# Branch A's product with w_branch_a moved out of the final stage, block by block, and half of w_out kept where h was

## The chip, the cores and the metric

The kernel runs on one core of one Trainium2 chip. The metric is device time in microseconds, the median of several executions. The core's engines are named as the profile names them: PE (TensorE, matrix products; PEld is its loading of weights), DVE (VectorE), ACT (ScalarE), POOL (GpSimd) and SP (SyncE, which here issues all the DMAs). SBUF is the on-chip memory, PSUM the memory that matrix products are written to.

## The reference

One layer of a hybrid encoder runs over a prompt of 2048 rows and a sample of 32 rows, with D_MODEL = 1024. Rows are normalised to h, and one projection of h gives everything else:

```python
qa, ka, va, za, qkv_b, zb, a_b, b_b, gate_a, gate_b = split_projection(x @ w_in)
oa = chunk_band_attention(qa, ka, va, rel_bias)             # branch A, 8 heads of 64
ya = (oa * silu(za)) @ w_branch_a                           # 512 -> 1024
ob, s_new = gated_delta_rule(qb, kb, vb, g, beta, s_prev)   # branch B, 8 heads of 64
yb = (ob * silu(zb)) @ w_branch_b                           # 512 -> 1024
mix = sigmoid(gate_a) * ya + sigmoid(gate_b) * yb
y = layer_norm(ALPHA * x + mix @ w_out, ln_g, ln_b)         # w_out is 1024 x 1024
```

The new keys, values, convolution rows and states are returned as well.

## The kernel before, in words

**Precision.** Products with w_in are made of fp16 pairs (a high and a low part of each operand, three products). Products with w_branch_a, w_branch_b and w_out are made of fp32r pairs in the same way: `hi*hi`, `hi*lo` and `lo*hi`.

**Order of the work.** The rows are done in two halves of 1024. For each half a list of jobs runs on PE (`all_jobs`, line 2051); a job is one 128-column piece of w_in against the half's rows. The jobs feed branch B (`phase_b`, 832), then attention (`phase_a`, 1501), and the last jobs of the second half are the gates of branch A. Each gate's tanh is stored in DRAM (`job_gate`, 813; `sig_dram`), and so are the two branches' gated outputs before their products (`g_dram`). The weights of a job come through two places (`raw_gate`, line 615) filled by `fetch` (618) and split into fp16 pairs by `divide` (662).

**A planner writes the program.** Each step is a Python generator. A small model (`Flow`, 157) gives every operation a cost and every engine a time when it is next free, and always continues the stream whose clock is lowest. Gates, marks and queues (84 to 155) order the streams. What comes out is one fixed list of instructions for each engine, and each engine works its list off in order, so a wait on one instruction holds up all behind it. Since `Engine.__getattr__` issues everything, every compute instruction has line 267 in the profile, and every DMA line 290; they are told apart by the tiles' names.

**The early products.** When the second half's branch B is done, w_branch_b is loaded (`load_w`, 640, called from `fetch`) and `early` (2222) makes branch B's products while attention of the second half runs. The rows are cut into eight blocks of 256 (the last has the 32 sample rows too). One *unit* is one block, one branch and one of eight 128-column pieces f: 12 matmuls (`branch`, 2264). `early` does two blocks at once in one PSUM bank `b`, multiplies by the gate on DVE and stores the result over the gate in `sig_dram`. It takes PE only when the planner sees it idle (line 2240), and it has three gate tiles (`SGB`).

**The final stage.** After the last jobs `fetch` loads w_branch_a to where h was (`hpool`), and `merge` (2278) goes over the blocks. For each f, `unit` makes branch A's product in bank `a` and multiplies by the gate; `fold` adds branch B's stored product and splits the sum into `mh` and `ml`; then four PSUM banks (two row tiles by two column halves, `pj` and `b`) collect 8 x 12 matmuls of 512 columns with w_out (`step`, `low`). A block's w_out products are interleaved with the next block's units (`LAG`). `finish` (2450) takes the banks on DVE, adds the normalised x rows and makes the second LayerNorm. The x rows come through three tiles `xt`: `x_load` (2431) normalises them on DVE and scales and shifts them on POOL, in 16 pieces of 256 columns a pair of tiles and factor.

w_out is split into fp32r pairs by `last_weights` (2099) once attention's memory is free (`fp_open`); it uses the x tiles and the four row vectors' tiles as staging. `q_sg` and `sg_ahead` (2403) load the gates and products through the three `sg` tiles.

**K rows in attention.** `job_k` (1652) writes the last 512 K rows out through one tile `kr`, guarded by `vs_slot`; other intermediates use four places `parts`.

Of the kernel before, what the change touches and what calls it, by code (L numbers as in the profile page):

```python
# [11 lines left out]
F32 = mybir.dt.float32  # L12
# [263 lines left out]
def trunk(ctx: ExitStack, tc: tile.TileContext, x_p, x_s, cache_k, cache_v, st_conv, st_gdn,  # L276
# [338 lines left out]
    raw_gate, w_gate, sig_slots = gate(NRAW), gate(2), gate(2)  # L615
    q_raw, q_w = Queue(flow), Queue(flow)

    def fetch(jobs):

        for job in jobs:  # L620
            if job.half == 1 and job.key == EARLY:
                yield from load_w(1, w_b)
            yield raw_gate
            raw = wpool.tile([P, KD, P], F32, tag="wraw", bufs=NRAW, name="wraw")
# [6 lines left out]
            q_raw.put((job, raw, t))  # L631
            yield

        jobs_near.done()
        yield from load_w(0, w_a)
        for _ in range(NRAW):
            yield raw_gate
        front_w.done()

    def load_w(br, w):  # L640
        yield from claim_w(br)
        for k in range(NP):
            yield raw_gate
            wr = wpool.tile([P, KD, P], F32, tag="wraw", bufs=NRAW, name="wr")
            wr = wr[:].rearrange("p k n -> p (k n)")
            t = dma(wr, w[k * P:(k + 1) * P, :])
            both = [None, raw_gate.give]
            for c in range(2):
                flow.start(split_w(br, k, c, wr[:, c * 512:(c + 1) * 512], t, both[c]))
            yield  # L650
# [11 lines left out]
    def divide():  # L662

        while True:
            job, raw, t = yield from q_raw.get()
# [17 lines left out]
            for i in range(2):  # L683
# [8 lines left out]
                if i:  # L692
                    raw_gate.give()
# [65 lines left out]
    wres, claimed = [None, None], [mark(), mark()]  # L759
# [12 lines left out]
    def split_w(br, k, c, wr, t, give=None):  # L772
        yield claimed[br]
        hi, lo = wres[br]
        yield from split(hi[c][:, k], lo[c][:, k], wr, give, V if k % 2 else G, t, w_ready[br, k, c])

    def claim_w(br):
        if br == 0:
            for g in h_free:
                yield g  # L780
        else:
            yield wr_open
        pool = wr_pool[0] if br else hpool
        names = [f"{x}{c}" for c in range(2) for x in ("hi", "lo")]
        ts = [pool.tile([P, NP, 512], F32R, tag=n, bufs=1, name=f"w{n}{br}") for n in names]
        wres[br] = [ts[0::2], ts[1::2]]
        claimed[br].done()
# [713 lines left out]
    def phase_a(half):  # L1501
# [8 lines left out]
        bias_slots, vs_slot, sample_slot = [gate(2), gate(1)], gate(1), gate(1)  # L1510
        last_block = len(BLOCKS[half]) - 1
        NPART = 4
# [139 lines left out]
        def job_k(k):  # L1652
# [10 lines left out]
            def evac(bi, c0, n, gcol, ps):  # L1663
# [4 lines left out]
                kr = None  # L1668

                def leave():  # L1670
                    nonlocal kr
# [23 lines left out]
                if kr is not None:  # L1695
                    yield from rows_out(kr, kr[:, 0:m], m, nk_p[c0 - (HALF - BAND):c0 - (HALF - BAND) + m], p,
                                        (k.k_s[:], nk_s) if m < n else None)
                    vs_slot.give()
# [227 lines left out]
        def leave_pair(k, t, gt, place):  # L1926
# [16 lines left out]
            at = dma(g_dram[0][k.p][:, cs], ga[:].rearrange("p i n -> p (i n)"))  # L1943
            if t == 6:
# [8 lines left out]
        def sample(k):  # L1953
# [78 lines left out]
            yield dma(g_dram[0][p][:, SEQ:T], ga[:])  # L2032
# [66 lines left out]
    def last_weights():  # L2099

        x_t = []
        for _ in range(3):
            yield x_slots
            x_t.append(fp.tile([P, D], F32, tag="xt", bufs=3, name="wr")[:])
        r_t = [rowv[name][:] for name in ("l0g", "l0b", "lng", "lnb")]

# [6 lines left out]
        def row(name, src):  # L2113
            for c in range(2):
                yield w_ready["o", 3 + list(rowv).index(name), c]
# [11 lines left out]
        stage = x_t + r_t  # L2127
        for i in range(2 * KD):
            if i >= 14:
                yield w_ready["o", 2, i % 2]  # L2130
            yield from load(i // 2, i % 2, stage[i // 2 if i < 14 else 2][:, i % 2 * 512:(i % 2 + 1) * 512])
# [3 lines left out]
        for k in (0, 1, KD - 1):  # L2135
# [11 lines left out]
    g_slot, g_early, x_slots = gate(1), gate(1), gate(3)  # L2147
    q_eg, q_eb, q_es = Queue(flow), Queue(flow), Queue(flow)
    q_eg.low = gate(0)
    early_done, claimed_b = [mark() for _ in range(NB)], {}  # L2150
    SGB = 3
# [5 lines left out]
    q_g, q_x, q_sg = Queue(flow), [Queue(flow), Queue(flow)], Queue(flow)  # L2157
# [21 lines left out]
    def load_g():  # L2179
        yield jobs_near  # L2180
        for b in range(NB):
            yield g_slot
            gs = [get_g(0, b, 0)]
            if not claim_block(b):
                yield g_early
                gs.append(get_g(1, b, 1))
            q_g.put(gs)
            yield

    def claim_block(b):  # L2190

        if b not in claimed_b:
            claimed_b[b] = "merge"
        return claimed_b[b] == "early"

    def early_g():
        yield wr_open
        for some in [[b, b + 1] for b in range(0, NB - 2, 2)] + [[NB - 2], [NB - 1]]:
            if some[0] in claimed_b or fp_open.at is not None:
                break  # L2200
            gs = []
            for i, b in enumerate(some):
                claimed_b[b] = "early"
                place = 1 - (b if len(some) == 1 else i)
                yield (g_slot, g_early)[place % 2]
                gs.append((b, get_g(1, b, place % 2), place % 2))
            q_eg.put(gs)
# [3 lines left out]
    def early_sg():  # L2211
        while True:
            c0, n = yield from q_eb.get()
            for f in range(KD):
                if c0 == SEQ // 2:
                    yield gate_done[1, 1, f]
                yield sg_slots
                sg = sg_tile()
                q_es.put((sg, dma(sg[:, 0:n], sig_dram[1][f][:, c0:c0 + n])))
# [359 lines left out]
```

## Time and profile before

| | |
|---|---|
| median of 3 executions | 2007.88 us (2007.57 to 2008.67) |
| the profiled execution | 2002.91 us, of which 2001.1 us span from first to last instruction |
| PE busy | 1903.8 us (95%) |
| DVE busy | 1410.8 us (70%) |
| ACT busy | 993.7 us (50%) |
| POOL busy | 807.2 us (40%) |
| mean granted TensorE clock | 0.978 |
| DMA | 257.57 MB, mean 129 GB/s |

A row of a group reads: line, engine, operation, tile written <- tiles read, shape, count | busy us, mean ns of one | idle time of the engine just before, and what ended most of it. A busy PE is not PE at its peak: matmuls overlap, so the time of one is read from the distance of their starts. A row of a stage reads: from:to, length, then busy us (and count) of PE, PEld, DVE, ACT and POOL, the granted clock, the busy share of the DMA engines and GB/s.

### The profile page before, as it was taken

The page shows a single profiled execution, that of the slowest core. Times are in us where ns is not written, and L with a number is a line of the kernel's source. Part 1 is how long each engine was busy: PE and PEld are TensorE (multiplying, and loading weights), DVE is VectorE, ACT ScalarE, POOL GpSimd, SP SyncE. Part 2 cuts the span into 40 slices and gives each one's busy share as a digit, 9 for nine tenths or more (in the row PEclk, how much of TensorE's full clock was granted, in tenths as well). Part 3 has the DMA queues.
Part 4 walks back from the last instruction along what each step waited for, and adds up shares of the span by engine and source line. Part 5 has one row for each costly group of instructions (what it writes and reads, how often), then busy time and mean ns, then how long its engine had stood idle before and what let it go on. Part 6 is the DMA issues. An engine that isn't in the chain of part 4 may idle for free.

```text
span 2001.1 us, 40919 instructions
## 1 busy us (share of the span) xinstructions
PE 1903.8 (95%) x14513; PEld 1347.3 (67%) x14513; DVE 1410.8 (70%) x4482; ACT 993.7 (50%) x2022; POOL 807.2 (40%) x1139
## 2 busy tenths in 40 slices
PE   8999999999999999999999999899999897799997
PEld 5455676676454557666676778588877566688885
DVE  7789989873378768589889985455366655676766
ACT  6665545444577777655445444444365764211110
POOL 7344434423344445343334432322132323456664
PEclk8999999999999999999999999999999998899998
DMA  3224232333478885222232342678688867544432
GB/s 132 67 88 128 63 105 67 90 94 97 122 158 197 185 185 141 76 77 80 60 109 65 89 109 75 172 190 207 204 176 201 160 152 189 203 145 136 149 128 78
DMA packets 371861, 257.57 MB, mean 129 GB/s; under 512 B 247106, under 2 KB 314030, under 8 KB 371656
## 3 DMA queue, kind: packets, MB, share of 16 engines
q1 hardware_dynamic: 371656, 254.96, 47.9%
q8 instruction: 114, 1.87, 0.4%
q14 instruction: 91, 0.75, 0.1%
HBM read 148.63 MB, written 63.24 MB: 106 GB/s over the span
## 4 chain that ended last, share of the span: by engine, by line
PE 66%; DVE 19%; ACT 5%; issue 4%; POOL 2%; DMA 2%; SPq 1%; POOLq 0%; DVEq 0%; ACTq 0%
PE pj L267 38%; PE b L267 14%; PE a L267 7%; PE x L267 3%; DVE acc L267 2%; PE c L267 2%; DVE sys_t L267 2%; DVE sys_u L267 2%; PE o L267 2%; DVE kd_bd L267 1%; POOL wlo L267 1%; DVE q_bd L267 1%; ACT whi L267 1%; POOL xt L267 1%; DVE v_t L267 1%
## 5 line engine op out<-in xcount | busy, mean ns | idle before, releaser
L267 PE MATMUL pj<-hi,whi 128*128 128x512 f16 (+2 forms) x1992 | 644.3, 339 | 18.8 <-ACT kr L267 8.9
L267 PE MATMUL pj<-hi,wlo 128*128 128x512 f16 (+2 forms) x1952 | 636.3, 339 | 0.6 <-POOL wlo L267 0.5
L267 PEld LDWEIGHTS <-whi 128*128 128x128 f16 x3984 | 410.0, 105 | 229.7 <-issue 12.3
L267 PE MATMUL pj<-lo,whi 128*128 128x512 f16 (+2 forms) x1992 | 457.0, 340 | 0.0
L267 POOL TENSOR_TENSOR wlo<-wraw,whi 128x256 f16<-128x256 f32 x384 | 268.8, 723 | 445.5 <-ACT whi L267 335.9
L267 PEld LDWEIGHTS <-wlo 128*128 128x128 f16 x1952 | 205.1, 105 | 120.7 <-issue 12.8
L267 ACT ACTIVATE wraw<-wraw,w_scale 128x1024 f32<-128x1024 f32 (+1 forms) x98 | 111.4, 1137 | 81.5 <-DVE w_scale L267 79.9
L267 POOL TENSOR_TENSOR pu<-sb,pu 128x640 f16<-128x640 f32 (+2 forms) x64 | 82.6, 1292 | 168.1 <-ACT pu L267 127.1
L267 ACT ACTIVATE sb<-sb,mx,unit 128x640 f32<-128x640 f32 (+4 forms) x128 | 108.7, 849 | 70.5 <-DVE mx L267 63.6
L267 ACT CAST whi<-wraw 128x512 f16<-128x512 f32 (+1 forms) x196 | 119.2, 610 | 35.2 <-PE pj L267 32.4
L267 DVE TENSOR_TENSOR sys_u<-sys_u,sys_t 128x60 f32<-128x60 f32 (+24 forms) x527 | 124.5, 242 | 5.7
L267 ACT CAST mh<-sg 128x256 fp32r<-128x256 f32 x64 | 25.7, 407 | 206.4 <-DVE sg L267 183.0
L267 DVE SCALAR_TENSOR_TENSOR acc<-raw,cwT,acc 128x512 f32<-128x512 f32 x144 | 112.8, 784 | 8.4 <-ACT acc L267 7.0
L267 DVE TENSOR_TENSOR sys_t<-sys_u,sys_p 128x60 f32<-128x60 f32 (+21 forms) x459 | 110.2, 243 | 5.5
L267 DVE CUSTOM_DVE_ANT_0 sb<-a,bias 128x320 f32<-128x320 f32 (+5 forms) x136 | 66.3, 498 | 50.3 <-PE a L267 48.9
L267 ACT COPY v_t<-o 128x64 f32<-128x64 f32 x132 | 27.8, 210 | 143.5 <-PE o L267 107.0
L267 POOL TENSOR_TENSOR w_scale<-w_scale,mhalf 128x1 f32<-128x1 f32 x49 | 32.1, 655 | 159.1 <-DVE w_scale L267 119.9
L267 PEld LDWEIGHTS <-pt 128*128 128x128 f16 x1680 | 67.3, 99 | 29.7 <-DMA pt<-pu 7.2
L267 ACT CAST pu<-sb 128x640 f16<-128x640 f32 (+4 forms) x128 | 82.0, 649 | 0.5
L267 ACT ACTIVATE sig<-pj,w_half 128x512 f32<-128x512 f32 (+2 forms) x84 | 49.3, 587 | 65.5 <-PE pj L267 60.0
L267 PE MATMUL c<-vt,pt 128*128 128x64 f16 x1680 | 70.9, 194 | 10.7 <-DVE ob L267 5.8
L267 PE MATMUL a<-ghi,whi 128*128 128x256 f32 (+1 forms) x256 | 68.3, 296 | 12.8 <-ACT ghi L267 7.6
(353 smaller groups left out, 4305.3 us busy)
## 6 DMA issues: line engine op xcount, KB each, us to landing
wraw<-in_w_in SPq DMA_DIRECT2D x192, 256.0 KB
sg<-sig SPq DMA_DIRECT2D x120, 128.0 KB
sig<-sig SPq DMA_DIRECT2D x44, 256.0 KB
sys_p<-sol_p SPq DMA_DIRECT2D x68, 128.0 KB
x<-in_x_p SPq DMA_DIRECT2D x16, 512.0 KB
xt<-in_x_p SPq DMA_DIRECT2D x16, 512.0 KB
out_y_p<-xt SPq DMA_DIRECT2D x16, 512.0 KB
glo<-g SPq DMA_DIRECT2D x14, 512.0 KB
```

The source lines that it names most:

```text
L267: r = f(*a, **k)
```

## The change

- Branch A's products become early units too. `early_g` lists branch B's five groups of blocks, then branch A's; a block of A waits until attention has written all four head pairs of it (`turned`), and its gates of the second half until they are stored (`gate_done`). w_branch_a takes w_branch_b's place when B's last unit is done (`load_a`). Once the final pool is open, the early units use six tiles `sl` in place of the three `sg`, and no longer wait for an idle PE.
- `fetch` ends with rows 0 to 511 of w_out, split into h's place (`load_o`); `last_weights` loads the other half, staged in the x tiles and one row vector's tile.
- `merge` keeps only the sum of two stored products (`load`, `fold`, five tiles `sf`) and the products with w_out. It uses banks `a`, `a`, `a`, `c` while units are still made, and then alternates between those and `pj`, `pj`, `b`, `b`.
- There are five x tiles instead of three. The K rows use the `parts`, of which the second half has five, instead of `kr` and its slot. The two places for raw weights are numbered, so that any stream can hand one back.

```diff
@@ weights
-        yield from load_w(0, w_a)
+        yield from load_o()
...
+    def load_o():
+        for g in h_free:
+            yield g
+        for i in range(2):
+            for name, some in zip(("hi", "lo"), wo):
+                t = hpool.tile([P, 2, D], F32R, tag=f"{name}{i}", bufs=1, name=f"wo{name}{i}")
+                some += [t[:, 0], t[:, 1]]
+        for k in range(KO):
+            yield from load_rows(w_out, k, lambda c: [x[k][:, c * 512:(c + 1) * 512] for x in wo],
+                                 lambda c: w_ready["o", k, c])
+
+    def load_a():
+        yield early_b
+        yield from load_w(0, w_a)
@@ K rows
-                        yield vs_slot
-                        kr = ap.tile([P, 3 * P], F32, tag="kr", bufs=1, name="kr")
+                        kr_place = yield from part_slots.take()
+                        kr = parts[kr_place][:].rearrange("p i n -> p (i n)").bitcast(F32)
@@ early units
     def early_g():
         yield wr_open
-        for some in [[b, b + 1] for b in range(0, NB - 2, 2)] + [[NB - 2], [NB - 1]]:
-            if some[0] in claimed_b or fp_open.at is not None:
-                break
+        units = [(1, some) for some in ([0, 1], [2, 3], [4, 5], [6], [7])]
+        units += [(0, some) for some in ([0, 1], [2, 3], [4, 5], [6], [7])]
+        n = 0
+        for br, some in units:
             gs = []
+            for b in some:
+                if br == 0:
+                    for p in range(NP):
+                        yield turned[b // 4, p, b % 4]
...
     def early_sg():
         while True:
-            c0, n = yield from q_eb.get()
+            br, c0, n = yield from q_eb.get()
             for f in range(KD):
-                if c0 == SEQ // 2:
-                    yield gate_done[1, 1, f]
-                yield sg_slots
-                sg = sg_tile()
+                if c0 >= SEQ // 2:
+                    yield gate_done[1, br, f]
+                if fp_open.at is None:
+                    slots = sg_slots
+                    yield slots
+                    sg = sg_tile()
+                else:
+                    slots = sl_slots
+                    yield slots
+                    sg = fp.tile([P, 2 * FB], F32, tag="sl", bufs=NSL, name="sl")
@@ merge
+        def load():
+            for B in blocks:
+                for f in range(KD):
+                    for br in range(2):
+                        yield early_done[br, B.b, f]
+                    yield sf_slots
+                    sg = fp.tile([P, 2, FW], F32, tag="sf", bufs=NSF, name="sf")
+                    for br in range(2):
+                        t = dma(sg[:, br, 0:B.n], sig_dram[br][f][:, B.b * FB:B.b * FB + B.n])
+                    flow.start(fold(B, f, sg, t))
+                    yield
...
-        for f in range(KD):
-            yield from unit(blocks[0], f)
-        for B, after in zip(blocks, blocks[1:]):
-            pss = {}
+        flow.start(load())
+        turn_ = 1
+        for B in blocks[:-1]:
+            turn_ = 0 if early_over.at is None else 1 - turn_
+            names, pss = (("aa", "ac"), (("pj", "pj"), ("b", "b")))[turn_], {}
             for t in range(2):
                 for c in range(2):
-                    pss[t, c] = yield from product(B, t, c)
+                    yield bank[names[t][c]]
+                    pss[t, c] = pt(names[t][c])
             for k in range(KD):
                 for (t, c), ps in pss.items():
                     yield from step(B, t, c, k, ps)
                 for (t, c), ps in pss.items():
                     yield from low(B, t, c, k, ps)
                 m_slots[k].give()
-                if k == KD - 1:
-                    yield from rows(B, (0, 1))
-                    for (t, c), ps in pss.items():
-                        end(B, t, c, ps)
-                if k >= LAG:
-                    yield from unit(after, k - LAG)
-            for f in range(KD - LAG, KD):
-                yield from unit(after, f)
+            yield from rows(B, (0, 1))
+            for (t, c), ps in pss.items():
+                end(B, t, c, ps, names[t][c])
@@ x rows, w_out
-        w.xt = xt = fp.tile([P, D], F32, tag="xt", bufs=3, name="xt")
+        w.xt = xt = fp.tile([P, D], F32, tag="xt", bufs=5, name="xt")
...
-    wo = [[fp.tile([P, D], F32R, name=f"wo{x}{k}") for k in range(KD if x == "h" else KD - 2)] for x in "hl"]
+    late_wo = [[fp.tile([P, D], F32R, name=f"wo{x}{k}") for k in range(KO, KD)] for x in "hl"]
```

More of the change, by code (lines that the diff above doesn't have):

```diff
@@ L614, in trunk @@
     NRAW = 2
-    raw_gate, w_gate, sig_slots = gate(NRAW), gate(2), gate(2)
+    raws = [wpool.tile([P, KD, P], F32, name=f"wraw{i}") for i in range(NRAW)]
+    raw_slots, w_gate, sig_slots = places(NRAW), gate(2), gate(2)
     q_raw, q_w = Queue(flow), Queue(flow)
@@ L664, in divide @@
         while True:
-            job, raw, t = yield from q_raw.get()
+            job, raw, place, t = yield from q_raw.get()
             if job.own:
@@ L2103, in last_weights @@
             yield x_slots
-            x_t.append(fp.tile([P, D], F32, tag="xt", bufs=3, name="wr")[:])
-        r_t = [rowv[name][:] for name in ("l0g", "l0b", "lng", "lnb")]
+            x_t.append(fp.tile([P, D], F32, tag="xt", bufs=5, name="wr")[:])
         def load(k, c, half):
@@ L2125, in scale @@
                 rows_ready.done()
[L2127 to L2131, printed above, removed]
+        stage = x_t + [rowv["lnb"][:]]
+        for i in range(2 * KO, 2 * KD):
+            yield from load(i // 2, i % 2, stage[i // 2 - KO][:, i % 2 * 512:(i % 2 + 1) * 512])
         for name, src in (("l0g", ln0_g), ("l0b", ln0_b)):
@@ L2534, in trunk @@
     ms = fr.tile([P, KD, 2 * DEC], F32R, name="ms")
-    wo[1] += [fr.tile([P, D], F32R, name=f"wol{k}") for k in range(KD - 2, KD)]
+    for some, more in zip(wo, late_wo):
+        some += more
     rowv = {}
```

225 lines of the change are left out of this document (81 added, 144 removed).

## The prediction

> **What bounds the kernel now.** I read the slices of the page first, then the busy times by stage, then who TensorE waits for in each stage, then the chain. The page:
>
> ```profile
> span 2001.1 us, 40919 instructions
> PE   8999999999999999999999999899999897799997
> PEclk8999999999999999999999999999999998899998
> L267 PE MATMUL pj<-hi,whi 128*128 128x512 f16 (+2 forms) x1992 | 644.3, 339 | 18.8 <-ACT kr L267 8.9
> ```
>
> TensorE is the bound for nearly all of the span. The slices that drop below 9 late in the run (two 7s with a clock of 8, and the end) are where the last attention ends and the final stage begins, at about 1674 us. The table of busy times by stage puts numbers on it (columns: PE, weight loads, DVE, ACT, POOL, clock, DMA share, GB/s):
>
> ```profile
> 1300.00:1540.00 240.00, 239.17 (x2154) 192.55 (x2152) 127.95 (x392) 115.78 (x240) 59.25 (x68) 1.00 0.79 195
> 1540.00:1600.00 60.00, 55.07 (x519) 36.63 (x517) 40.10 (x143) 44.13 (x86) 17.43 (x19) 1.00 0.80 171
> 1600.00:1674.00 74.00, 73.20 (x687) 50.49 (x688) 40.65 (x143) 44.67 (x92) 20.51 (x22) 0.98 0.62 145
> 1674.00:1730.00 56.00, 34.25 (x225) 29.94 (x222) 38.02 (x71) 22.02 (x42) 25.08 (x21) 0.74 0.84 269
> 1730.00:1950.00 220.00, 220.00 (x1256) 193.74 (x1255) 142.84 (x256) 29.87 (x82) 128.18 (x149) 1.00 0.41 134
> ```
>
> From 1300 to 1674 PE has almost no hole; branch B's early products already sit there (1300 to 1540) and cost no wait. From 1674 to 1730 it is busy 34 of 56 us, at a granted clock of 0.74. From 1730 to 1950 it has no hole at all. Who is late in the hole, and the only DVE wait before it:
>
> ```profile
> PE a L267 <- ACT ghi L267: 7.6, 1, 7.6
> PE c L267 <- DMA pt<-pu: 4.6, 1, 4.6
> ...
> PE pj L267 <- DVE ql L267: 2.5, 1, 2.5
> ```
>
> The last transposes of attention, then the load of the second g block, which stands on the SP queue behind the gate, weight and x loads: the stage has nothing else for PE to do. So the rule of the sum: **moving PE work does not remove it. The change can gain only what PE idles now**, less what the new order makes it idle.
>
> **The idle that can be had, step by step.** The price of a unit (12 matmuls of 256 columns of one branch, one f) and of a w_out matmul come from the chain (start, us, what); the last row is the time in which a gate tile lands:
>
> ```profile
> 1749.80 4.24 PE a L267 x36
> 1774.82 1.43 PE a L267 x12
> 1916.58 4.24 PE a L267 x36
> 1925.38 0.23 PE pj L267
> ...
> 1699.77 4.48 DMA sg<-sig
> ```
>
> A unit is 1.43 us. From 1749.80 to 1916.58 are five equal blocks, 33.36 us each; 8 units take 11.4, which leaves 21.9 us for 96 w_out matmuls, 0.228 each (the 0.23 row). The work that PE really did from 1674 to 1730 is by count (six w_out groups of 7, 7, 7, 6, 6, 6; first and last shown):
>
> ```profile
> L267 PE MATMUL a<-ghi,whi 128*128 128x256 f32 x36 | 12.6, 368 | 12.8 <-ACT ghi L267 7.6 <-DVE sg L267 5.2
> L267 PE MATMUL pj<-wol,mh 128*128 128x512 f32 x7 | 3.0, 424 | 0.0
> L267 PE MATMUL b<-woh,ml 128*128 128x512 f32 x6 | 2.3, 389 | 0.0
> ```
>
> Nine units (three groups of 36) are 12.9 us, 39 w_out matmuls 8.9, the end of attention a few more (I take 3): 25 of 56 us. **Lost: 31 us.** After 1950:
>
> ```profile
> L267 PE MATMUL pj<-wol,mh 128*128 128x512 f32 x16 | 6.3, 391 | 0.0
> L267 PE MATMUL b<-woh,ml 128*128 128x512 f32 x18 | 4.7, 389 | 0.0
> L267 PE MATMUL pj<-woh,ms 128*64 128x512 f32 x8 | 4.0, 504 | 4.9 <-POOL ms L267 3.3 <-DVE ms L267 1.6
> L267 PE MATMUL a<-ghi,whi 128*128 128x288 f32 x12 | 3.3, 296 | 0.0
> 1990.30 1.97 PE L267 MATMUL b<-woh,ml 128*128 128x512 f32 x8
> ```
>
> Four groups of 16, two of 18 and four of 8 (the sample rows) are 132 w_out matmuls, 30.1 us, and three units with 288 columns some 4.8; the last matmul ends at 1992.3. So 35 of 42 us. **Lost: 7 us**, in waiting for the folds. What follows (8.8 us to the end of the span: evacuation, row statistics, two passes over the row, the store) stays.
>
> In phase A the 8.9 us behind `kr` (one tile for the K rows; the group row above) go if each of two K blocks finds a part of its own, and the 2.5 us behind `ql` are covered if a unit of A stands there: 11 us. Five parts instead of four, with up to three for v, one and now two for k and two for the sample, can also be short: between 0 and 11 us, I take 9. Together **31 + 7 + 9 = 47 us can be had.**
>
> **What the new order costs.** The moved work: 64 units on PE (8 blocks of 11.4 us, no cheaper, no dearer), 32 evacuations of 512 columns and some of 256 on DVE, the splits of eight g blocks and of w_a on ACT, DVE and POOL, and on SP one more load and one more store of every A gate (2080 columns by 1024 rows, 8.5 MB each way). Before 1674 there is no room on PE for more than the few holes; a unit that the planner puts there delays gates by as much as it takes from later, so I cost it at nothing: B's units in 1300 to 1540 ran at DMA share 0.79 and PE 239 of 240 us. If that cover were gone, a wait for a gate tile (4.48 us) per pair of units over 16 pairs would be the price of A's first four blocks, 72 us; no B pair shows one.
>
> The added waits stand on SP: a gate load of blocks 4 to 7 waits for that gate's store, a final load for the store of A's product. Behind them in the queue stand attention's transposes, then x loads and row stores, and the folds wait for those. A landing is 4.48 us; five load tiles ahead of the folds cover it, so nothing; uncovered, one landing in each of blocks 4 to 7, 18 us.
>
> From 1674 until the final pool opens (about 1691, after the last transposes) A's pairs have three gate tiles. A tile's round is a load of 4.48 us, a pair of 2.85, an evacuation under 1 and a store like the load: some 12 us, so a pair every 4 us where PE needs 2.85. PE is short by 30% of 17 us: 5. From 1691 six tiles serve, but then w_out's second half (2 MB), four row vectors (2 MB) and five x tiles (2.5 MB) come, with 269 GB/s now in this stage as a whole. At that rate 6.8 MB (decimal) take 25 us; A's pairs would want 0.52 MB per 2.85 us beside them. The half of w_out in h's place is there by then and lets PE do the first four k of a block, 11 us. Between 0 (loads and units side by side) and 14 us (25 less 11): I take 9, nearer the top since DMA share is 0.84 there already. **Transition: 14 of the 31 us stay.** The rest of w_out, which was on the path (its last lo half before the first block can be finished), is then hidden under A's remaining units; the cover is at least the 46 us of blocks 4 to 7, which cannot start before their gates, the last jobs.
>
> In the steady blocks PE falls from 33.36 to 21.9 us, and the question is who else needs more. POOL and DVE over the same five blocks, and POOL alone (the last three rows, from the time line):
>
> ```profile
> L267 POOL TENSOR_TENSOR xt<-xt,l0g 128x256 f32<-128x256 f32 x40 | 31.3, 820 | 22.9 <-DVE xt L267 22.9
> L267 POOL TENSOR_TENSOR xt<-xt,l0b 128x256 f32<-128x256 f32 x34 | 27.3, 837 | 0.0
> L267 POOL TENSOR_TENSOR ml<-sg,mh 128x256 fp32r<-128x256 f32 x20 | 19.6, 980 | 33.7 <-ACT mh L267 33.7
> L267 POOL TENSOR_TENSOR m<-m,mhalf 128x1 f32<-128x1 f32 x10 | 9.7, 968 | 15.5 <-DVE m L267 15.5
> ...
> L267 DVE TENSOR_TENSOR sg<-sg 128x256 f32<-128x256 f32 x40 | 21.8, 553 | 0.7
> L267 DVE SCALAR_TENSOR_TENSOR sg<-sg,a 128x256 f32<-128x256 f32 x40 | 16.6, 415 | 44.5 <-PE a L267 20.2 <-DMA sg<-sig 13.1 <-POOL xt L267 11.3
> L267 DVE SCALAR_TENSOR_TENSOR xt<-xt,m,lnb 128x1024 f32<-128x1024 f32 x10 | 15.1, 1515 | 0.0
> L267 DVE SCALAR_TENSOR_TENSOR xt<-xt,m,lng 128x1024 f32<-128x1024 f32 x10 | 13.2, 1324 | 0.0
> L267 DVE TENSOR_TENSOR ml<-sg,mh 128x256 fp32r<-128x256 f32 x20 | 9.0, 451 | 8.2 <-ACT mh L267 8.2
> ```
>
> ```profile
> 1981.79 5.62 POOL L267 TENSOR_TENSOR xt<-xt,l0b 128x256 f32<-128x256 f32 x8
> 1921.36 0.74 POOL L267 TENSOR_TENSOR ml<-sg,mh 128x256 fp32r<-128x256 f32 x1
> 1922.06 0.55 POOL L267 TENSOR_TENSOR m<-m,mhalf 128x1 f32<-128x1 f32 x1
> ```
>
> Each alone is below 21.9: POOL keeps (31.3 + 27.3 + 19.6 + 9.7) / 5 = 17.6 us a block. But look at the pairs of numbers: m takes 0.55 alone and 0.97 in the mean, ml 0.74 and 0.98, the DVE add of two SBUF tiles 0.55 where the evacuation of the same width, which reads PSUM, takes 0.42. POOL and those DVE operations hold each other up. If they can never overlap, a block needs their sum. From below: POOL 16 × 0.70 + 4 × 0.74 + 2 × 0.55 = 15.3; DVE 8 × 0.42 + 4 × 0.45 + 4 × 1.32 = 10.4; together 25.7, or 3.8 over PE's 21.9. It counts only where no unit of A is left to fill PE, some five blocks: 19 us; five x tiles instead of three let about two be prepared ahead, 2 × 8 × 0.70 = 11. I take 7 us (between 0 and 19).
>
> In the Trainium skill, "SBUF — State Buffer", section "Who interferes with whom", says that a DVE instruction with two SBUF inputs and a GpSimd instruction that reads SBUF exclude each other for their whole length. The stretched rows agree. By that rule kept in all eight blocks 8 × 3.8 = 30 us would be lost where I take 7; that is rival 5.
>
> **Sum.** 47 − 14 − 7 = 26 us less. The profiled execution took 2002.91 us (span 2001.1), the median of the runs is 2007.88, 5 us above it; I take the difference off the median: **1982 us**.
>
> **The rivals.** (1) *POOL and DVE become the bound of all eight blocks* (slower). From above, with the durations as they stand, waits included: 17.6 + (21.8 + 15.1 + 13.2 + 9.0) / 5 = 29.4 a block. Halfway between the two sums, 27.5, is 5.6 over PE; eight blocks lose 45 us against 47 − 14 = 33 gained: 2008 − 33 + 45 = 2020. It decides from 21.9 + 33 / 8 = 26 us a block. For it: the stretched rows, and that the rule's lower sum already stands at 25.7. Against: A's units fill PE in the first blocks, and the means count waits twice. 0.13. (2) *The transition stays as it is*: DMA share 0.84 leaves A's pairs without gate tiles until the weights are in, so all 31 us stay; 47 − 31 − 7 = 9 less, 1999. 0.17. (3) *Nothing new is paid*: the transition costs 5 and port contention 0; 42 less, 1966. For it, PE's 239 of 240 us beside B's units; 0.20. (4) *It does not do what it says*: no unit of A is placed before 1674, since the planner waits for idle PE. That is not slower by itself: the same units then fill the hole; it is inside the forecast. (5) *Strict exclusion at the lower sum*, 25.7 in all eight blocks: 30 us lost against 33, 2005, no difference that shows; 0.05.
>
> **How the numbers follow.** Forecast (1972 to 1992) 0.45; rivals 0.13, 0.17, 0.20, 0.05. A measurement here can tell about 0.2%, 4 us. Faster by more: 0.45 + 0.17 + 0.20 = 0.82; same 0.05; slower 0.13. The range runs from nothing at all paid and all 11 us of phase A had (2008 − 49 = 1959) to just above the second rival: 1958 to 2002, which leaves out rivals 1 and 5.
>
> **What would show it.** Right: PE near 56 of 56 us in the 56 us after the last job, at clock 1.00; no wait for `kr`; one `b` group with A's weights in two places, before and after the last job; steady blocks of 22 to 25 us; an end of 9 us after the last matmul. Wrong: blocks of 26 us or more with PE waiting for `ml` or for a bank that DVE frees late, and POOL or DVE without idle time; PE waiting for `sg` loads after 1674; attention ending much later while PE idles, which would mean that units stood in front of it without their data.

## The result, and the profile after

The changed kernel takes 1982.72 us (median of 4 executions, 1980.36 to 1986.43), the kernel before beside it 2007.72 us (2004.79 to 2008.67): a ratio of 0.988, interval 0.9861 to 0.9898. That is 25.0 us less; 1982 was predicted.

| | before | after |
|---|---|---|
| the profiled execution | 2002.91 us | 1980.36 us |
| its span | 2001.1 us | 1978.6 us |
| PE busy | 1903.8 us | 1894.8 us |
| POOL busy | 807.2 us | 814.7 us |
| mean granted TensorE clock | 0.978 | 0.988 |
| DMA | 257.57 MB | 274.62 MB |

The slices of the page after, and its first group of instructions:

```profile
PE   8999999999999999999999999999999999989996
PEclk9999999999999999999999999999999999999998
L267 PE MATMUL pj<-hi,whi 128*128 128x512 f16 (+2 forms) x1992 | 642.3, 338 | 11.2 <-DVE zb L267 3.2
```

The two 7s of the transition are gone, and so is `kr`. A single 8 near the end is new: something is late there that was not before. The busy times by stage of the changed kernel (from:to, length, PE, weight loads, DVE, ACT, POOL, clock, DMA share, GB/s):

```profile
1674.00:1730.00 56.00, 54.37 (x430) 48.82 (x428) 29.12 (x53) 19.14 (x43) 18.02 (x17) 1.00 0.96 295
1730.00:1950.00 220.00, 203.24 (x1031) 169.74 (x1031) 168.50 (x265) 29.23 (x78) 144.07 (x163) 0.95 0.56 186
1910.00:1950.00 40.00, 30.43 (x115) 21.17 (x114) 27.97 (x47) 3.67 (x14) 28.75 (x34) 0.83 0.33 108
```

From 1674 to 1730 PE is now busy 54.4 of 56 us at clock 1.00 (34.25 at 0.74 before). But from 1730 to 1950, where it had no hole, it now idles 16.8 us, in two places: around 1760 and around 1930. Who PE waits for from 1680 to the end (total us, times, longest):

```profile
PE a L267 <- DVE xt L267: 6.0, 1, 6.0
PE b L267 <- POOL ms L267: 5.9, 1, 5.9
PE b L267 <- DVE ms L267: 3.6, 1, 3.6
```

The first is a bank: block 0's products fill `a`, `a`, `a`, `c`, and the units made in between leave only this set of banks. The evacuation of block 0 adds the x rows, and they are not ready. In both kernels DVE scales and shifts the rows of the first two tiles itself; POOL does it for all later tiles, in eight pieces a tile. The time line of DVE there (start, us):

```profile
1746.11 1.43 DVE L267 TENSOR_TENSOR xt<-xt,l0g 128x256 f32<-128x256 f32 x4
...
1753.30 3.60 DVE L267 TENSOR_TENSOR xt<-xt,l0g 128x256 f32<-128x256 f32 x4
...
1761.31 3.54 DVE L267 TENSOR_TENSOR xt<-xt,l0b 128x256 f32<-128x256 f32 x4
...
1767.17 0.67 DVE L267 SCALAR_TENSOR_TENSOR xt<-a,xt 128x512 f32<-128x512 f32 x1
```

and POOL at the same time:

```profile
1751.99 7.27 POOL L267 TENSOR_TENSOR xt<-xt,l0g 128x256 f32<-128x256 f32 x8 [7.77 <-DMA sf<-sig]
```

DVE scales tile 0 from 1746 and shifts tile 1 only at 1761; the same four pieces take 1.43 us while POOL stands idle (up to 1751.99) and 3.6 once it scales rows of its own. Only at 1767.17 is the third bank taken, and PE goes on, at a granted clock of 0.50 from 1767.9 to 1770. The second place is the last block. First POOL (the bracket says what ended the idle time before):

```profile
1915.02 9.04 POOL L267 TENSOR_TENSOR xt<-xt,l0g 128x256 f32<-128x256 f32 x4 [2.08 <-DVE xt L267]
1924.02 0.25 POOL L267 TENSOR_TENSOR ms<-sf,ms 128x32 fp32r<-128x32 f32 x1
1924.23 2.80 POOL L267 TENSOR_TENSOR xt<-xt,l0g 32x256 f32<-32x256 f32 x4
```

The first of these rows is four pieces. The second piece by itself (the same time line, 1918 to 1919.5):

```profile
1915.87 6.80 POOL L267 TENSOR_TENSOR xt<-xt,l0g 128x256 f32<-128x256 f32 x1
```

SP's loads, and what SP waits for from 1900 to 1950 (total us, times, longest):

```profile
1909.51 16.54 SPq L290 DMA_DIRECT2D sf<-sig  x10
SPq L290 <- POOL ms L267: 19.3, 2, 11.6
```

DVE:

```profile
1919.58 2.46 DVE L267 SCALAR_TENSOR_TENSOR xt<-xt,m,lnb 128x1024 f32<-128x1024 f32 x2
1927.14 2.49 DVE L267 TENSOR_TENSOR sf<-sf 128x288 f32<-128x288 f32 x2 [4.43 <-POOL xt L267]
```

Read it as a circle. POOL does its list in order, so `ms` at 1924.02, 0.25 us of work, stands behind four row pieces that take 9.04 us. Nearly all of that is one piece: the second is held from 1915.87 to 1922.67, while DVE works off nine operations without a gap between them (from 1915.23 to 1922.71, four passes over the row among them, 1.27 us each at most). The last two pieces take 0.73 us each. Until `ms` is done, an `sf` tile stays occupied; of SP's ten loads, which need these tiles, six are out by 1912.6 and the seventh leaves at 1924.30; DVE stands 4.43 us until 1927.14, and the folds that PE needs come late. Behind PE's waits the granted clock is 0.50 again, from 1940.7 to 1944. The sample rows take four pieces per factor too, though they fill 32 partitions only. The steady blocks between the two stalls, by one row of the chain each:

```profile
1816.50 1.40 PE a L267 x6
1838.56 0.93 PE pj L267 x4
1860.65 1.39 PE a L267 x6
```

22.1 us from block to block, PE's own 21.9, though the strict sum of POOL and DVE was 25.7.

### The profile page after: what moved, and what is told of

It is laid out like the page before. It is cut to its first block, busy times and chain, and to the rows that moved or that the text cites. A ratio compares the mean times of both kernels' runs of the same rounds, so it can differ in the third digit from the quotient of the medians.

```text
span 1978.6 us, 41065 instructions
## 1 busy us (share of the span) xinstructions
PE 1894.8 (96%) x14513; PEld 1338.2 (68%) x14513; DVE 1421.8 (72%) x4458; ACT 993.2 (50%) x2022; POOL 814.7 (41%) x1139
## 2 busy tenths in 40 slices
DMA packets 382806, 274.62 MB, mean 139 GB/s; under 512 B 248322, under 2 KB 319342, under 8 KB 382600
## 4 chain that ended last, share of the span: by engine, by line
PE 64%; DVE 20%; issue 5%; ACT 4%; DMA 4%; POOL 3%; SPq 1%; POOLq 0%; DVEq 0%; ACTq 0%
PE pj L267 34%; PE b L267 15%; PE a L267 7%; PE c L267 4%; PE x L267 3%; DVE acc L267 3%; DVE sys_t L267 2%; DVE sys_u L267 2%; PE o L267 2%; DVE kd_bd L267 1%; POOL wlo L267 1%; SPq L290 1%; DVE xt L267 1%; DVE q_bd L267 1%; DMA sf<-sig 1%
## 5 line engine op out<-in xcount | busy, mean ns | idle before, releaser
L267 PE MATMUL pj<-hi,whi 128*128 128x512 f16 (+2 forms) x1992 | 642.3, 338 | 11.2 <-DVE zb L267 3.2
L267 POOL TENSOR_TENSOR wlo<-wraw,whi 128x256 f16<-128x256 f32 (+1 forms) x392 | 280.6, 738 | 460.9 <-ACT whi L267 380.5
L267 PE MATMUL b<-ghi,whi 128*128 128x256 f32 (+1 forms) x512 | 138.7, 303 | 3.6 <-DVE cr L267 1.1
L267 ACT CAST whi<-wraw 128x512 f16<-128x512 f32 (+2 forms) x212 | 128.2, 611 | 27.5 <-PE pj L267 24.6
L267 PE MATMUL b<-ghi,wlo 128*128 128x256 f32 (+1 forms) x512 | 129.5, 284 | 0.0
L267 ACT CAST mh<-sf 128x256 fp32r<-128x256 f32 x64 | 25.7, 406 | 178.8 <-PE c L267 74.8
L267 PEld LDWEIGHTS b<-ghi,whi 128*128 128x128 f32 x512 | 97.3, 190 | 9.7 <-ACT ghi L267 1.5
L267 PEld LDWEIGHTS b<-ghi,wlo 128*128 128x128 f32 x512 | 97.5, 190 | 1.5
```

The costliest lines, as they stand in the source:

```text
L267: r = f(*a, **k)
```

## The experiments

**Theory:** the gain is PE's idle time filled, and what is left of it (the two stalls) is made by the scaling and shifting of the x rows on POOL beside DVE. **Rivals:** the gain comes from the early start of A's units, or from the K rows; the stalls come from slots and landings of the loads.

**e1_kr_alone.** The kernel before with only the K rows' part of the change:

```diff
-                        yield vs_slot
-                        kr = ap.tile([P, 3 * P], F32, tag="kr", bufs=1, name="kr")
+                        kr_place = yield from part_slots.take()
+                        kr = parts[kr_place][:].rearrange("p i n -> p (i n)").bitcast(F32)
...
-        NPART = 4
+        NPART = 4 + last
```

> The kernel before with one part of the change alone: the K rows use the parts, of which the second half has five, instead of one tile kr. Theory (the change gains only what PE idles): PE's waits for kr, 8.9 us in before, go, some of it comes back as waits for parts, and everything after moves forward: 5 us less, ratio 0.9975 (0.996 to 0.999). Rival (phase A is bound by its latency chain and not by PE): ratio 1.000. Rival (most of the change's 25 us comes from here): 0.990.

Ratio 0.9993, interval 0.998 to 1.0006 (2006.65 us): no difference that shows. PE's waits from 1250 to 1690 in it:

```profile
PE pj L267 <- ACT part L267: 9.6, 3, 5.7
```

The wait of 8.9 us behind `kr` has become one of 9.6 behind `part`: with this edit alone the place changes its name, not its lateness.

**e2_late_a.** The changed kernel, with A's units held back until all jobs are done:

```diff
         for br, some in units:
+            if br == 0:
+                yield jobs_done
```

> The changed kernel, but no product of branch A starts before the last job's matmuls (in the changed kernel 13 of its 64 units do). Theory (moved PE work only pays where PE would idle): the jobs end 18 us earlier, near 1669 us, the 13 units are made later, and the time stays within 6 us of the changed kernel's, ratio to before 0.987 to 0.991. Rival (being early is what pays): the 18 us are lost, ratio 0.996 to 0.998.

Ratio 0.9897 (0.9883 to 0.9912), 1985.71 us: nearly all of the gain is there without one early unit, and the two intervals overlap. A's product is a filling for the transition, and its early start is worth at most some 3 us. The last job's last matmul starts at 1665.1 us here and at 1687.5 in the changed kernel, 22.4 us apart: 16 of A's 64 units lie in between, not the 13 of the expectation (the count is shown further below).

**e3_x3.** The changed kernel with three x tiles (`bufs=3`, `gate(3)`) in place of five.

> The changed kernel with three x tiles instead of five. Theory (POOL and DVE fall behind in the short blocks, and tiles ahead of need are what hides it): steady blocks longer than 22.1 us, with PE waiting for banks, 15 to 30 us more than the changed kernel, ratio to before 0.995 to 1.003. Rival (x tiles do not matter, as in before where three did): within 4 us, 0.986 to 0.990.

Ratio 0.9911 (0.9898 to 0.9923), 1989.04 us: between the two, nearer to the rival. The tiles are worth about 6 us by the medians (the intervals touch), and the wait for the bank grows:

```profile
PE a L267 <- DVE xt L267: 9.3, 2, 7.2
```

**e4_no_pool_rows.** The changed kernel without POOL's pieces. From row 256 on it leaves out the factor and the addend of the first LayerNorm in the residual; all else stays.

```diff
-            for q in range(4):
+            for q in range(4 if gt < 2 else 0):
```

> The changed kernel without the scale and shift of x rows 256 and up on POOL (it leaves out ALPHA times ln0_g and ln0_b there). Theory (the 14 us that PE stands still before the last block come from POOL's row work, in whose queue the folds wait): that stall shrinks to under 3 us, ratio to before 0.980 to 0.984; the 6 us wait for a bank near 1762 us stays in part. Rival (the five sf tiles and their loads make it): the stall stays over 10 us and the time within 4 us of the changed kernel's, 0.986 to 0.990.

Ratio 0.9795 (0.9778 to 0.9813), 1964.24 us, 18.5 us below the changed kernel by the medians of two comparisons (17 by the ratios), a little more than the theory's bracket. The stages that had the stalls:

```profile
1730.00:1950.00 220.00, 216.25 (x1109) 182.39 (x1108) 153.78 (x282) 30.40 (x81) 52.09 (x57) 0.99 0.60 198
1910.00:1950.00 40.00, 40.00 (x176) 30.96 (x175) 31.91 (x54) 3.15 (x12) 11.16 (x14) 1.00 0.31 105
```

PE has 40.0 of 40 us at the end, where it had 30.4, and the wait for bank `a` is no longer in the list. DVE makes more operations in this stage than in the changed kernel (282 against 265), yet it is busy 153.8 us instead of 168.5: some of the time that DVE shows in the changed kernel is POOL's hold-up. The theory holds, and for both stalls: the expectation had left part of the first one standing. That run says what the row work costs, not how to avoid it; the next ones look for that.

**e5_sf7.** Two more tiles for the folds' loads: `NSF` 5 to 7 (and `NSL` 6 to 4, for the memory).

> The changed kernel with seven sf tiles instead of five (and four sl tiles instead of six, for room). Theory (before the last block the folds wait in POOL's queue behind its row work): the stall before the last block stays over 7 us and the time within 5 us of the changed kernel's, ratio to before 0.986 to 0.991. Rival (the round from a fold to a free sf tile to the next load sets the end): the stall is under 3 us, ratio 0.980 to 0.984.

Ratio 0.9895 (0.9869 to 0.9921), 1988.69 us: nothing gained. PE's waits from 1660 on:

```profile
PE b L267 <- DVE sl L267: 11.6, 2, 10.6
PE b L267 <- POOL ms L267: 6.2, 1, 6.2
```

The second row is the end: 6.2 us where it was 9.5 in the changed kernel, under the theory's 7 and far above the rival's 3. So more slots take a third of that wait; they are not what makes it. The 10.6 us are the first stall, grown from 6.0: PE waits until 1774.59 for a bank that DVE frees behind its x rows. Whether that comes from the two `sl` tiles that this run takes away, no run tells.

**e6_ports.** The disputed cost by itself: not the layer at all but 16 POOL products of 128x256, alone and beside one kind of DVE operation at a time (it computes nothing of the reference).

> No layer at all: 16 POOL products of 128x256 alone, five DVE operations alone, and each of them beside the POOL products; the outputs are left unwritten except for zeros. Theory (POOL and a DVE operation with two SBUF inputs cannot overlap): the add of two SBUF tiles and the 1024-column row pass with two SBUF inputs take together with POOL the sum of the two times alone, and the stage with the PSUM operand and the statistics take only the longer of the two. Rival (they share bandwidth or do not meet): both together take less than 1.3 times the longer. The 1024-column scaling, one SBUF input, is open: either.

The time line, each row one block of equal instructions (start, us, count); the short operations that start a block and the two blocks of row statistics are left out:

```profile
5.72 12.76 POOL L303 TENSOR_TENSOR p_pool_alone<-pa,pb 128x256 f32<-128x256 f32 x16
19.27 7.30 DVE L306 TENSOR_TENSOR v_add_alone<-va,vb 128x256 f32<-128x256 f32 x16
27.19 21.12 DVE L306 TENSOR_TENSOR v_add_both<-va,vb 128x256 f32<-128x256 f32 x32
27.32 13.84 POOL L303 TENSOR_TENSOR p_add_both<-pa,pb 128x256 f32<-128x256 f32 x16
48.93 10.04 DVE L309 SCALAR_TENSOR_TENSOR v_row_alone<-va,vb 128x1024 f32<-128x1024 f32 x8
59.59 16.19 DVE L309 SCALAR_TENSOR_TENSOR v_row_both<-va,vb 128x1024 f32<-128x1024 f32 x10
59.72 21.46 POOL L303 TENSOR_TENSOR p_row_both<-pa,pb 128x256 f32<-128x256 f32 x16
82.03 11.57 DVE L312 SCALAR_TENSOR_TENSOR v_evac_alone<-ps,vb 128x512 f32<-128x512 f32 x16
94.22 11.57 DVE L312 SCALAR_TENSOR_TENSOR v_evac_both<-ps,vb 128x512 f32<-128x512 f32 x16
94.35 12.80 POOL L303 TENSOR_TENSOR p_evac_both<-pa,pb 128x256 f32<-128x256 f32 x16
133.88 8.71 DVE L318 TENSOR_SCALAR v_scale_alone<-va 128x1024 f32<-128x1024 f32 x12
143.21 13.13 DVE L318 TENSOR_SCALAR v_scale_both<-va 128x1024 f32<-128x1024 f32 x12
143.33 16.80 POOL L303 TENSOR_TENSOR p_scale_both<-pa,pb 128x256 f32<-128x256 f32 x16
```

Beside the evacuation, which reads PSUM, nothing stretches: 12.80 and 11.57 us, as alone. The same holds beside the row statistics (POOL 12.78 us, DVE 11.63 alone and together). Beside passes over the row POOL goes from 12.76 to 21.46 us, and DVE from 1.26 a pass (10.04 / 8) to 1.62. If the two excluded each other wholly, ten passes and 16 products would need 12.55 + 12.76 = 25.3 us; they were done in 21.6 (59.59 to 81.18). 32 adds and 16 products would need 27.4 and took 21.1. So the hold-up is real and large, but partial here: neither the theory's sum nor the rival's 1.3 times the longer one. (The kernel itself has a case that is not partial, the piece of 6.80 us above.)

**e7_sample_dve.** The sample's 32 rows scaled and shifted on DVE (`eng = V if gt < 2 or gt == SEQ // P else G`).

> The changed kernel with the sample rows' scale and shift on DVE instead of POOL: 5.7 us of POOL become 2.9 us of DVE just before the last block. Theory (POOL's row work delays the last folds): the stall before the last block shrinks by 3 to 6 us, ratio to before 0.984 to 0.987. Rival: no change, 0.987 to 0.990.

Ratio 0.9855 (0.9836 to 0.9874), 1979.74 us: inside the theory's bracket, though the interval overlaps that of the changed kernel. PE's wait behind POOL's `ms` is 5.5 us where the end had 9.5.

**e8_sum_early.** The sum of the two branches' products made on DVE with A's product, so that later folds load one tile instead of two.

```diff
+                    if sb is not None:
+                        V.tensor_tensor(out=sg[:, 0:n], in0=sg[:, 0:n], in1=sb[:, 0:n], op=ALU.add)
+                        yield
```

> The changed kernel, but once the final pool is open the sum of the two branches is made with A's product (one more load and a 512-column add per pair of blocks there) and the fold of those blocks loads one tile and adds nothing; four sl tiles with four more beside them, eight half tiles sf. Theory (DVE's adds of two SBUF tiles hold up POOL in the short blocks): 8 x 0.42 us a block less to share, so the stall before the last block falls to under 6 us; the early stretch pays up to 4 us for its loads; ratio to before 0.983 to 0.987. Rival (loads in the early stretch cost more than the end gives): 0.989 to 0.995.

Ratio 0.9882 (0.986 to 0.9904), 1984.75 us: between the brackets, no gain. PE's waits from 1660 on, the longest first, and those after 1900:

```profile
PE b L267 <- DVE sl L267: 13.3, 1, 13.3
...
PE b L267 <- POOL ms L267: 0.9, 1, 0.9
```

Half of the theory holds: with fewer adds on DVE, and eight half tiles for the folds' loads, the end waits 0.9 us, not 9.5. What is won there is lost elsewhere. The first stall, over at 1775.32, is 13.3 us instead of 6.0, and 12.6 us follow the last matmul instead of 8.4. This run, too, has four `sl` tiles where the changed kernel has six.

**e9_rows_first.** The row vectors and the first x tiles loaded ahead of w_out's second half:

```diff
         stage = x_t + [rowv["lnb"][:]]
-        for i in range(2 * KO, 2 * KD):
-            yield from load(i // 2, i % 2, stage[i // 2 - KO][:, i % 2 * 512:(i % 2 + 1) * 512])
         for name, src in (("l0g", ln0_g), ("l0b", ln0_b)):
             yield from row(name, src)
         flow.start(x_ahead())
+        for i in range(2 * KO, 2 * KD):
+            yield from load(i // 2, i % 2, stage[i // 2 - KO][:, i % 2 * 512:(i % 2 + 1) * 512])
```

> The changed kernel, with the two row vectors l0g and l0b and the first x tiles loaded ahead of the second half of w_out. Theory: the stall of 6 us near 1761 us, with TensorE at half clock behind it, comes from x rows that are scaled and shifted too late, because their row vectors land only at 1726 and 1736 us; some 8 us earlier they take 4 to 8 us off it: ratio 0.984 to 0.986 (the changed kernel has 0.988). Rival: the transfers of this stage only change places, the second half of w_out comes later instead and the first blocks wait for it: 0.987 to 0.991.

Ratio 0.9899 (0.9875 to 0.9922), 1986.41 us: a miss. PE's waits after 1660:

```profile
PE a L267 <- POOL ms L267: 10.3, 3, 7.0
PE a L267 <- ACT woh L267: 3.1, 1, 3.1
...
PE a L267 <- DVE xt L267: 0.5, 1, 0.5
```

The first stall is gone as the theory said (6.0 to 0.5), 3.1 come back as a wait for w_out, as the rival said, 3.5 as two waits for the early units' `sl` and `glo`, and the end is 11.2 us (POOL and DVE `ms`) where it was 9.5. So what is won at block 0 is waited out elsewhere; the end stall stays while POOL does the row work.

**e10_odd_dve.** Every second tile and the sample take no POOL pieces; DVE does them in two passes, the form that the second LayerNorm has already:

```diff
+        if gt % 2 or gt == SEQ // P:
+            V.scalar_tensor_tensor(out=xt[:rows], in0=xt[:rows], scalar=mv[:rows, gt, 0:1],
+                                   in1=rowv["l0g"][:rows], op0=ALU.subtract, op1=ALU.mult)
+            yield
+            V.scalar_tensor_tensor(out=xt[:rows], in0=xt[:rows], scalar=mv[:rows, gt, 1:2],
+                                   in1=rowv["l0b"][:rows], op0=ALU.mult, op1=ALU.add)
+            yield
+            w.ready.done()
+            return
```

> The changed kernel, with the x rows of every second tile and of the sample made on DVE in two passes over the row, (x - mean) * l0g and (. * rstd) + l0b, in place of one DVE pass and eight POOL pieces. Theory: POOL's row pieces in front of the last folds make the stalls at 1928 and 1936 us (about 13 us with the clock behind them). A tile costs POOL 5.6 us less and DVE about 1.7 us more (two passes of 1.22 for one of 0.69), so DVE stays below TensorE's 22.1 us a block and most of the end stall goes: 0.981 to 0.985. Rival: DVE is as full as POOL (168 of 220 us), and two passes more in a block make it the bound: 0.988 to 0.995.

Ratio 0.9863 (0.9838 to 0.9887), 1975.77 us: between the brackets. The end stall is mostly gone (POOL `ms` 2.7 us), and a wait of 4.9 us for a `glo` split on DVE is new.

**e11_both.** e9 and e10 together, tiles 0 and 1 on DVE in two passes too.

> Both edits: the row vectors first, and the rows of tiles 0 and 1, of every second tile and of the sample on DVE in two passes. Theory: the two stalls are separate and both go, 0.977 to 0.982, near the run without POOL's row work (0.9795). Rival: one stall only moves into the other, as after taking POOL's rows of the sample away: 0.984 to 0.988.

Ratio 0.9846 (0.9822 to 0.9871), 1974.0 us: inside the rival's bracket. In the same comparison it is 12.4 us under e9, so most of this is e10's edit.

**e12_all_dve.** The row vectors first, all x rows on DVE in two passes (the condition is `True`), and every `ml` on POOL (`eng = G` in `fold`).

> The row vectors first, all x rows on DVE in two passes, and all the low parts ml on POOL, which then does no row work at all. Theory: DVE's own sum for a block is 8 adds of 0.40, 4 evacuations and 4 row statistics of 0.68 each, 8 row passes of 1.22: 18.4 us, with small ones about 20, below TensorE's 22.1, and nothing but 8 ml of 0.74 on POOL to collide with: 0.977 to 0.983. Rival: DVE with 20 of 22.1 us has no room for lateness and becomes the bound of the last blocks: 0.985 to 0.995.

Ratio 0.9822 (0.98 to 0.9845), 1969.74 us, 16.7 below e9 on the same chip: inside the theory's bracket, and the fastest of the kernels that compute everything. Its stages:

```profile
1730.00:1950.00 220.00, 213.83 (x1097) 179.39 (x1097) 175.31 (x251) 33.54 (x89) 94.34 (x93) 0.99 0.60 197
1910.00:1950.00 40.00, 40.00 (x176) 30.93 (x175) 36.77 (x53) 4.08 (x16) 19.20 (x21) 1.00 0.29 99
```

PE has no hole in the last of these stages; what it still waits for is w_out's second half (3.8 and 1.2 us, ahead of 1740). DVE is busy 175.3 of 220 us, 7 more than in the changed kernel: it has room for two row passes a tile instead of one, because POOL holds it up less and took its `ml`. The changed kernel itself was not in this comparison, and the kernel before varied more in it than beside the result (1999.1 to 2011.44); against the changed kernel's own median it is 13 us less.

## Why the prediction was right, and where its terms were not

The time came out as predicted, and the rule behind it held: moving PE work does not remove it, only PE's idle time can be had. The sum can be closed on the traces, between three marks: the last product of branch B, the last job's last matmul and the last matmul of all. (Rows: count, least, median and greatest ns, first and last start.) The end of branch B before, after and in e2:

```profile
L267 PE MATMUL o<-vn,qk_bd x36: 219/275/323, 1200.1 to 1241.4; 128*128 128x64 f32 x36
L267 PE MATMUL o<-vn,qk_bd x32: 219/275/323, 1201.5 to 1237.2; 128*128 128x64 f32 x32
L267 PE MATMUL o<-vn,qk_bd x36: 219/275/323, 1201.6 to 1243.0; 128*128 128x64 f32 x36
```

The last job before, after and in e2:

```profile
L267 PE MATMUL pj<-lo,whi x32: 279/279/280, 1660.2 to 1672.8; 128*128 128x272 f16 x32
L267 PE MATMUL pj<-lo,whi x24: 279/279/279, 1676.9 to 1687.5; 128*128 128x272 f16 x24
L267 PE MATMUL pj<-lo,whi x64: 279/279/390, 1622.1 to 1665.1; 128*128 128x272 f16 x48, 128*128 128x512 f16 x16
```

A's units ahead of it (four of these matmuls a unit), and the last matmuls of after:

```profile
L267 PE MATMUL b<-ghi,whi x64: 276/282/392, 1635.1 to 1681.5; 128*128 128x256 f32 x64
1969.16 1.08 PE L267 MATMUL a<-woh,ml 128*128 128x512 f32 x4
```

So 16 of A's 64 units, 22.9 us at 1.43, lie ahead of the last job in the changed kernel. From the last job to the end of the last matmul (1992.3 and 1970.2) are 319.5 and 282.7 us. Before, 31 + 7 of these were lost by the prediction's count, so 281.5 are work. After, 258.6 are work and 24.1 are lost: 13.9 us gained. From the end of branch B to the last job are 431.4 us before and 450.3 after, 18.9 more for 22.9 us of units: 4.0 gained. The end after the last matmul is 0.4 shorter. That is 18.3; the spans differ by 22.5, since the changed kernel's profiled execution was already 4.2 us ahead when branch B ended. In the other traces with the change that mark lies from 1241.7 to 1248.5, not before the 1241.4 of before, so these 4.2 us are scatter and not the change.

- **Transition and end: 38 to be had, 14 + 7 to stay.** 24 stayed, close to the 21 forecast, but not for the reasons given. With the last job at 1691.2 and the last matmul's end at 1955.2, e4, with the same 16 units ahead, loses 5.4 in this stretch, so 18.7 of the 24 are POOL's row work, and the medians say 18.5.
- **The transition: 14 of 31 us to stay.** The forecast mechanism, gate tiles that starve behind w_out's loads, did not show: PE is busy 54.4 of 56 us with a DMA share of 0.96. What stayed is a bank that waits for x rows, which the prediction did not have: it asked who needs the transfers, not who takes block 0's banks. Shared out by the lengths of the waits (6.0 and 9.5 us, an estimate) some 9 of the 24 belong to it. No run separates A's units as a filling from the half of w_out that is now there early; both fill this stage.
- **The end and the ports: 7 to be had, 7 paid.** By the same estimate the end lost 15 us, where it had lost 7; so this term was about 8 us too good. The prediction looked for the price of the ports in the pace of the steady blocks, and there it was nothing (22.1 us a block); it came where the list runs out, when POOL's row pieces stand in front of the last folds. e4 shows the cause. e5 shows that more slots do not take it away, e12 that the row work on DVE does.
- **Phase A: 9 us.** The size was right and the reason only in part. Without A's units in it (e2) the stretch from the end of branch B to the last job is 422.1 us, 9.3 less than before. But the K rows alone gave nothing (e1): there the wait of 9.6 us went to the next owner of the same memory, while in e2 it is 1.8 and in the changed kernel 1.3. Which other part of the change is needed stays open. The wait behind `ql` is down from 2.5 to 1.7, and to 1.4 in e2, where no unit of A covers it.
- **A's units before 1674 at nothing.** Right in the total: between e2 and the changed kernel no difference shows that is clear of the intervals. In the traces the 16 units make phase A 28.2 us longer (1.76 each, not 1.43) and shorten what follows by 27.5.
- **The landings on SP, w_out hidden.** Right as far as it went: PE waits for no part of w_out, except where its second half is pushed back (e9, 3.1 us; e12, 3.8). SP's late loads at the end wait for tiles (19.3 us behind `ms`), hardly for stores (2.4).
- **The rivals.** POOL and DVE as the bound of all blocks did not happen, nor strict exclusion at 25.7 us a block. The Trainium skill, "SBUF — State Buffer", section "Who interferes with whom", calls the pair of ports that the two engines share an exclusive lock. The numbers of e6 agree as to which operations collide and show less than a full block in the total (21.6 us against 25.3); the piece of 6.80 us in the kernel is a full one, through nine operations.

So from the end of branch B on this pair of traces gives 18.3 us where 26 were forecast: some 5 more from the transition, 8 less at the end, and 5 less in phase A, because A's units there cost more than their price. The errors cancel in part only. The spans differ by 22.5 us with the scatter, the medians by 25.0 (20.5 to 27.9 by the interval). That the rule held and the size is near 20 us is the prediction's merit; that the median came within 1 us of it is luck.

## What to carry to other kernels

When an engine that is the bound is given filling work, count its idle time, not the work that is moved; then ask, at the first and at the last block of the new stage, who frees its banks and who stands ahead in each list. A slot that shows as the releaser is not yet a gain: its wait can go to the next owner of the place. Where POOL and DVE share a stage, it can pay to give DVE a whole two-pass form, even when DVE is the busier of the two, rather than to split a row between them.

## What the runs showed of the hardware

- 16 POOL products of 128x256 take 12.76 us alone, 13.84 beside adds of two SBUF tiles, 21.46 beside passes over a row, 16.80 beside a DVE operation with one SBUF tile and two scalars, 12.78 beside row statistics, and 12.80 beside an evacuation from PSUM. The DVE operation with one tile was not in the prediction's picture: the normalisation `xt<-xt,mv` is of that kind, and it collides (8.71 to 13.13 us for twelve). The Trainium skill, "SBUF — State Buffer", section "Who interferes with whom", says that `tensor_scalar` can run in a mode that contends with GpSimd; the run agrees in that it collides.
- Where they collide in e6, POOL and DVE take turns, one operation each. Beside the adds an add and a product start every 0.87 us (alone every 0.46 and 0.80). Beside the row passes a pass and a product start about every 1.66 us (alone every 1.26 and 0.80); the median product lasts 1.58 us and the median pass 1.63. So the engine with the shorter operations loses more.
- In the changed kernel POOL got no turn: one product lasted 6.80 us, through nine DVE operations, and DVE's passes took 1.27 us, as alone. In e6 some 0.03 us lie between two passes, which write the same tile; in the kernel the nine operations follow each other without a gap. Whether the gap is what lets POOL in, no run shows.
- The granted clock of TensorE was 0.50 from 1767.9 to 1770 and from 1940.7 to 1944, right behind the two waits, and 1.00 again from 1774 and 1948 on.
